# Two-layer decoder trunk: layer 0's softmax weights moved by GpSimd DMAs into fp32r transposes, layer 1's values set directly behind its scores

## The chip, the cores and the metric

The kernel runs on one core of a Trainium2 chip. The core has a matrix engine (PE), a vector engine (DVE), a scalar engine (ACT), GpSimd (POOL) and a queue that issues most DMAs (SP). The metric is the device time of one execution in microseconds.

## The reference, cut to what matters

The input is one sequence of 256 positions by 1024 features in fp32. There are two layers, each an attention and a gated feed-forward network (up-projection to 2 x 2816 columns, a causal convolution of width 3, SiLU of the gate times the value, down-projection), with RMS norms before each and residual sums behind.

Layer 0's attention is dilated: for each of 16 heads of 64 dimensions there are three groups (window, dilation) = (128, 1), (512, 4), (2048, 16), each with its own q, k and v. The three are merged by their softmax denominators, which makes one softmax over the keys of all three. Layer 1's attention is causal over one block of 256 keys. In both, q and k are normalised and partly rotated before the scores:

```python
scores = einsum('rnqhd,rnkhd->rnhqk', q, k) * HEAD_DIM ** -0.5   # masked
p = exp(scores - m);  o = (p @ v) / p.sum(-1)                     # then the heads times w_o
```

## The kernel before, in words

Every large product is made in three fp32r matmuls: a weight tile `raw` is split by ACT into a rounded part `whi` (L109) and by DVE into the rest `wlo` (L117); the activations stand as such a pair in `xT`. `mm3` (L456 to L458) adds hi x hi, lo x hi and hi x lo in PSUM. These are the product matmuls, 512 columns each.

Attention runs over four sections of four heads. A section's product is a list of pieces; each piece is one **turn**, 12 product matmuls on PE (6 in the output product). `turn()` (L218 on) fixes the program's order: around each piece it runs what tables `first`, `pre`, `mid` and `post` hold for that turn, and `at(table, dt, f)` enters a step `dt` turns from now. Inside a turn the order is: the weight splits, `first`, one split by DVE, `pre`, the piece itself, `post`. In the first 80 turns `post` is sorted by `PART`. There is no scheduler behind it: every engine works strictly in the order in which the steps were recorded.

The softmax of four heads, for each half c of the positions, goes through these steps:

- **A** (`step_A`): PE makes the scores into banks named S. There are four such banks, handed out in turn. In layer 0 one A takes all four (one per head), in layer 1 two.
- **E** (`step_E`): DVE adds the mask and takes the maximum (L716, one call and one read of `mx` per head, which is what frees the bank), ACT takes exponentials (L725) into tiles `sm`.
- **R** (`step_R`): DVE scales by the reciprocal of the sum (L733).
- **T** (`step_T`): PE transposes the weights in blocks of 128 x 128 against `ident` into S banks (L741): 12 blocks and three banks in layer 0; in layer 1 four blocks and one bank for c = 0, two times four for c = 1.
- **V** (`step_V`): ACT copies them to tiles `pT` (L748).
- **C** (`step_C`): PE multiplies with the values (L773). It uses plain fp32, in which one matmul leaves two records in the profile. For sections 0 to 2 both halves c make one group, in the last section each half its own.
- `split_T` (L433) turns C's result into the hi and lo parts of `aT` (L444 on ACT, L445 on DVE), which the output product reads.

Where these steps stand is set by numbers: `PLANS` and `C_TURN` in layer 0, and `plan`, `odd`, `last` in layer 1 (c = 0 at turn 6, 5 or 7 of the section, c = 1 two turns later). T comes four turns behind A in layer 0 (two in the last section). `OUT_ORDER` orders the pieces of the output product. q and k of a section are transposed by L580 and copied by L610 (ACT) with low parts by L616 and L618 (DVE); POOL takes the powers for the norms (L318).

Of the kernel before, what the change touches and what calls it, by code (L numbers as in the profile page):

```python
# [40 lines left out]
PART_TURNS = 80  # L41
PART = {"step_C": 0, "step_A": 1, "step_T": 2, "transpose": 3}

# [13 lines left out]


def r32(ap):
    return ap.bitcast(F32)  # L60
# [81 lines left out]
def trunk_kernel(ctx, tc, x, a_w_qkv, a_w_o, b_w_qkv, b_w_o, ffn_norm, ffn_w_up, ffn_w_down, pack, mask_a, mask_b,  # L142
# [75 lines left out]
    def turn(fn, pump=2, crowded=False):  # L218

        t = now[0]  # L220
        end = len(ws.parts) if t >= LATE else None
        n = min(pump, 1 if len(ws.parts) - ws.taken >= AHEAD else 2)
        if not crowded:
            ws.start(n)
        for f, a in first.pop(t, ()):
            f(*a)
        ws.finish(1, end)
        for f, a in pre.pop(t, ()):
            f(*a)
        if crowded:  # L230
            ws.start(n)
        ws.finish(end=end)
        if fn is not None:
            fn()

        late = post.pop(t, [])
        if t < PART_TURNS:
            late.sort(key=lambda fa: PART.get(fa[0].__name__, len(PART)))
        for f, a in late:
            f(*a)  # L240
        now[0] += 1
# [12 lines left out]
    def gain_row(l):  # L254
        g = cp.tile([P, D], F32, name="gain", bufs=1)
        nc.gpsimd.dma_start(g, ffn_norm[l:l + 1, :].to_broadcast([P, D]))
        return g
# [10 lines left out]
    for i in range(WARM):  # L268
        nc.tensor.matmul(warm[:, 0:P], plain[:, 0:P], plain[:, 0:P], start=True, stop=True)
    ident = cp.tile([P, P], F32, name="ident")  # L270
    make_identity(nc, ident)
    ones = cp.tile([P, 1], F32, name="ones")
# [8 lines left out]

    pk = cp.tile([P, PK], F32, name="pk")
    nc.sync.dma_start(pk[:, 0:264], pack[:, 0:264])
    mA = cp.tile([P, 768], F32, name="mA")
    mB = cp.tile([P, 384], F32, name="mB")
# [3 lines left out]
    cwT = [pk[:, 264 + l * 176:440 + l * 176] for l in range(2)]  # L289
    CG = cp.tile([P, 2, 4, 2, 16], F32, name="CG")  # L290
# [142 lines left out]

    def split_T(dst, k0, nk, c, src_ps, spread=False):
# [9 lines left out]
        nc.scalar.activation(hi, s, AF.Copy)  # L444
        nc.vector.tensor_sub(lo, s, r32(hi))  # L445

# [14 lines left out]
    def attention(xT, norms, ng, g0, mask):  # L461
# [198 lines left out]

        O, weights, starts = {}, {}, []

        def step_A(sec, c, heads, qkT, v, rq):
# [41 lines left out]

        def step_E(c, heads, rq, place, n, part, sm, st):
# [5 lines left out]
            these = range(len(heads))[part]  # L712
            sm.extend(t[:, i * n:(i + 1) * n] for i in range(len(these)))
            for i in these:
                s2, o = place[i]
# [11 lines left out]

        def step_R(heads, sm, st, n):
            den = st[0]
            rd = sp.tile([P, 4], F32, name="rd", bufs=2)  # L730
            nc.vector.reciprocal(rd[:, 0:len(heads)], den[:, 0:len(heads)])
            for i in range(len(heads)):
                nc.vector.tensor_scalar(sm[i], sm[i], rd[:, i:i + 1], None, op0=ALU.mult)  # L733

        def step_T(sec, c, heads, v, sm, n):
            tot = n * len(heads)
            Tp = [ps.tile([P, 512], F32, name="S", bufs=4) for _ in range((tot + 511) // 512)]
            for b in range(tot // P):
                o = b % 4 * P
                i = b * P % n  # L740
                nc.tensor.transpose(Tp[b // 4][:, o:o + P], sm[b * P // n][:, i:i + P], ident)  # L741
            at(pre, 1, step_V, sec, c, heads, v, Tp, tot)

        def step_V(sec, c, heads, v, Tp, tot):
            pT = [bp.tile([P, 768], F32, name="pT", bufs=4) for _ in range((tot + 767) // 768)]
# [7 lines left out]
            if heads[-1] < HS - 1 and (whole or not dil) or whole and c == 0:  # L753
                weights[key] = held
            else:
                at(post, starts[sec] + C_TURN[sec] - now[0] if whole and dil else 1, step_C, sec, held)

        def step_C(sec, held):

            for c, heads, pT, v in held:  # L760
# [21 lines left out]
        else:  # L782
            plan, odd, last = ([(s, 0, (0, 1, 2, 3)), (s + 2, 1, (0, 1, 2, 3))] for s in (6, 5, 7))
        pumps = PUMPS if dil else (2, 0, 0, 2, 1, 2)
        vs = [[None, None] for _ in range(NSEC)]
        for sec in range(NSEC):
            qk, v, rq = [], vs[sec], {}
            starts.append(now[0])
            for s, c, heads in last if sec == NSEC - 1 else begin if dil and sec == 0 else odd if sec % 2 else plan:
                at(post, s, step_A, sec, c, heads, qk, v, rq)  # L790
# [240 lines left out]
    at(post, 12, nc.sync.dma_start, pk[:, 264:PK], pack[:, 264:PK])  # L1031
    at(post, 20, nc.sync.dma_start, mB, mask_b)
    aT = attention(xT, norms, NG, 0, mA)
    for c in range(2):
        nc.gpsimd.dma_start(xr[:, c, :], x[0, c * P:(c + 1) * P, :])
# [109 lines left out]
```

## Time and profile before

| what | value |
|---|---|
| runs | 761.17 us median of 3 (760.97 to 761.58) |
| profiled execution | 761.35 us |
| its span, first to last instruction | 759.6 us |
| PE busy | 754.9 us, 99% |
| DVE busy | 582.4 us, 77% |
| ACT busy | 506.3 us, 67% |
| POOL busy | 68.7 us, 9% |
| DMA traffic | 133.83 MB |

A row of instruction groups reads: line of the kernel, engine, operation, output<-inputs, shape, count; in the timeline, its start and length in microseconds stand in front, and in brackets behind the idle time of the engine before it and who ended that. PEld is the loading of PE's stationary operand, which overlaps matmuls. Matmuls are pipelined: the durations of neighbours overlap, so the pace is read from start to start.

### The profile page before, as it was taken

The numbers are of one execution on the slowest core, as the hardware profiler recorded it, in microseconds if no ns is written. First come the engines' busy times: TensorE is split into PE (matmuls) and PEld (weight loads), VectorE is DVE, ScalarE is ACT, GpSimd is POOL, SyncE is SP. The second block draws the span as 40 slices with busy tenths as digits, with TensorE's granted clock in tenths as the row PEclk, the third lists the DMA queues.
The fourth block names the chain that finished last, engine by engine and source line by source line (L and its number), as shares of the span: only waits on it lengthen the run. The fifth ranks groups of instructions, "written<-read, shape, count | busy, mean of one in ns | idle before, by whom it ended". The sixth has DMA issues, their size and how long they took to land.

```text
span 759.6 us, 12047 instructions
## 1 busy us (share of the span) xinstructions
PE 754.9 (99%) x4394; PEld 634.9 (84%) x4394; DVE 582.4 (77%) x1123; ACT 506.3 (67%) x887; POOL 68.7 (9%) x77
## 2 busy tenths in 40 slices
PE   9999999999999999999999999999999999999998
PEld 7888888888888888888888888888788888888886
DVE  7887875975786566997787786979866798877874
ACT  7788666757786457676656656878765677666660
POOL 0330120320121000000000001112000000000000
PEclk9999999999999999999999999999999999999999
DMA  9947452562746436487666553743646368666621
GB/s 295 332 145 248 132 183 82 180 219 61 231 164 217 132 90 200 141 247 223 192 188 178 195 189 115 245 139 112 191 115 191 113 200 240 196 179 198 193 97 56
DMA packets 149452, 133.83 MB, mean 176 GB/s; under 512 B 5904, under 2 KB 134544, under 8 KB 149392
## 3 DMA queue, kind: packets, MB, share of 16 engines
q1 hardware_dynamic: 148816, 130.96, 56.2%
q0 software_dynamic: 576, 2.10, 0.7%
q8 instruction: 34, 0.56, 0.3%
q14 instruction: 26, 0.21, 0.1%
HBM read 131.99 MB, written 1.05 MB: 175 GB/s over the span
## 4 chain that ended last, share of the span: by engine, by line
PE 98%; DMA 1%; SPq 0%; ACT 0%; DVE 0%; issue 0%
PE acc L896 14%; PE acc L456 13%; PE acc L458 13%; PE acc L457 13%; PE acc L899 8%; PE S L949 5%; PE S L950 5%; PE S L951 5%; PE O L896 5%; PE O L899 3%; PE O L773 2%; PE S L741 2%; PE acc L513 2%; PE acc L580 2%; PE S L682 1%; PE S L458 1%
## 5 line engine op out<-in xcount | busy, mean ns | idle before, releaser
L117 DVE TENSOR_TENSOR wlo<-raw,whi 128x1024 fp32r<-128x1024 f32 x236 | 283.8, 1218 | 6.9 <-ACT whi L109 6.6
L109 ACT ACTIVATE whi<-raw 128x1024 fp32r<-128x1024 f32 x236 | 244.3, 1054 | 5.9 <-DMA raw<-in_a_w_qkv_dram 2.3
L456 PE MATMUL acc<-whi,xT 128*128 128x512 f32 x424 | 171.7, 405 | 0.0
L458 PE MATMUL acc<-wlo,xT 128*128 128x512 f32 x424 | 165.9, 391 | 0.0
L457 PE MATMUL acc<-whi,xT 128*128 128x512 f32 x424 | 165.4, 390 | 0.0
L896 PE MATMUL acc<-xT,whi 128*128 128x512 f32 x480 | 119.3, 390 | 0.0
L896 PEld LDWEIGHTS acc<-xT,whi 128*128 128x128 f32 x480 | 88.3, 188 | 17.2
L458 PEld LDWEIGHTS acc<-wlo,xT 128*128 128x128 f32 x424 | 79.6, 188 | 17.5
L456 PEld LDWEIGHTS acc<-whi,xT 128*128 128x128 f32 x424 | 79.7, 188 | 16.7 <-issue 1.2
L457 PEld LDWEIGHTS acc<-whi,xT 128*128 128x128 f32 x424 | 79.8, 188 | 14.8
L318 POOL TENSOR_TENSOR rs_y<-rs_v,mhalf 128x8 f32<-128x8 f32 x32 | 52.7, 1646 | 210.9 <-DVE rs_v L316 208.0
L899 PEld LDWEIGHTS acc<-xT,wlo 128*128 128x128 f32 x480 | 65.5, 190 | 4.7
L949 PE MATMUL S<-whi,kT 128*128 128x512 f32 x174 | 68.2, 392 | 0.0
L950 PE MATMUL S<-whi,kT 128*128 128x512 f32 x174 | 68.1, 391 | 0.0
L951 PE MATMUL S<-wlo,kT 128*128 128x512 f32 x174 | 67.7, 389 | 0.0
L920 DVE SCALAR_TENSOR_TENSOR qk<-sm,pk,qk 128x255 f32<-128x255 f32 (+1 forms) x160 | 66.7, 479 | 0.4 <-ACT qk L917 0.3
L899 PE MATMUL acc<-xT,wlo 128*128 128x256 f32 x480 | 66.9, 282 | 0.0
L909 DVE TENSOR_TENSOR sm<-acc,pT 128x256 f32<-128x256 f32 x60 | 25.4, 424 | 46.9 <-ACT pT L908 46.9
L917 ACT ACTIVATE qk<-sm,pk 128x256 f32<-128x256 f32 x80 | 47.8, 598 | 4.0 <-DVE sm L909 3.7
L933 ACT ACTIVATE kT<-qk 128x512 fp32r<-128x512 f32 x22 | 13.9, 633 | 41.2 <-DVE qk L928 41.2
L896 PE MATMUL O<-xT,whi 128*128 128x512 f32 x160 | 40.2, 393 | 0.0
L951 PEld LDWEIGHTS S<-wlo,kT 128*128 128x128 f32 x174 | 32.7, 188 | 7.0
(167 smaller groups left out, 925.7 us busy)
## 6 DMA issues: line engine op xcount, KB each, us to landing
raw<-in_ffn_w_up_dram SPq DMA_DIRECT2D x80, 512.0 KB, 4.5
raw<-in_a_w_qkv_dram SPq DMA_DIRECT2D x144, 256.0 KB, 4.4
raw<-in_ffn_w_down_dram SPq DMA_DIRECT2D x44, 512.0 KB, 4.0
raw<-in_b_w_qkv_dram SPq DMA_DIRECT2D x48, 256.0 KB, 3.5
raw<-in_a_w_o_dram SPq DMA_DIRECT2D x8, 512.0 KB, 3.4
raw<-in_ffn_w_up_dram SPq DMA_DIRECT2D x16, 256.0 KB, 3.6
raw<-in_b_w_o_dram SPq DMA_DIRECT2D x8, 512.0 KB, 4.0
xr<-in_x_dram POOLq DMA_DIRECT2D x2, 512.0 KB, 5.8
```

What stands on the lines that cost most here:

```text
L109: self.nc.scalar.activation(hi, raw, AF.Copy)
L117: self.nc.vector.tensor_sub(lo, self.raw[self.done], r32(hi))
L318: nc.gpsimd.tensor_tensor(y, v, mhalf[:, 0:n], op=ALU.pow)
L456: nc.tensor.matmul(acc, T[:, k, 0, cs], hi, start=first, stop=False)
L457: nc.tensor.matmul(acc, T[:, k, 1, cs], hi, start=False, stop=False)
L458: nc.tensor.matmul(acc, T[:, k, 0, cs], lo, start=False, stop=last)
L896: nc.tensor.matmul(acc, hi[:, k], xT[:, k].rearrange("p j t -> p (j t)"), start=(k == 0), stop=False)
L899: nc.tensor.matmul(acc[:, S:2 * S], lo[:, k], xT[:, k, 0], start=False, stop=(k == 7))
L920: nc.vector.scalar_tensor_tensor(o[:, d:S], u[:, 0:S - d], cw[:, first_tap + b:first_tap + b + 1], o[:, d:S], op0=ALU.mult, op1=ALU.add)
L949: nc.tensor.matmul(o, acts[f][:, 0, cs], hi[:, sl], start=start, stop=False)
L950: nc.tensor.matmul(o, acts[f][:, 1, cs], hi[:, sl], start=False, stop=False)
L951: nc.tensor.matmul(o, acts[f][:, 0, cs], lo[:, sl], start=False, stop=stop)
```

## The change

Layer 0, sections 0 to 2: behind R a new step M copies the tiles `sm` by GpSimd DMAs into tiles `pL` that are declared fp32r (384 KB each, two per step, so twelve in all); the bits are copied unchanged. T then transposes `pL` with an fp32r identity. T stands later: five, seven and six turns behind A for c = 0 in sections 0, 1 and 2, and six for c = 1. The last section and layer 1 keep fp32 transposes out of `sm`.

Layer 1: both score steps of section 0 stand in one turn. Values of sections 0 and 1 are entered so that they stand directly behind the next section's scores (`early`), those of section 2 behind the last section's second scores, where a new sorting of `post` puts A ahead of C. The last section's values make one group. R is entered ahead of other steps of its turn. The lo part of `aT` is made one turn after the hi part for sections 0 to 2. Two pieces of the output product change places.

To make room, the gain row takes a buffer of `kT`, the small pack one of `pT`, the two masks share one buffer, the identity is drafted in a buffer of `qk` and copied once by DVE, and layer 1's gain tables are made at turn 12, not 40.

```diff
-PART = {"step_C": 0, "step_A": 1, "step_T": 2, "transpose": 3}
+PART = {"step_C": 0, "step_A": 1, "step_T": 2, "transpose": 3}, {"step_A": 0, "step_C": 1}
...
-        if t < PART_TURNS:
-            late.sort(key=lambda fa: PART.get(fa[0].__name__, len(PART)))
+        part = PART[t >= PART_TURNS]
+        late.sort(key=lambda fa: part.get(fa[0].__name__, len(part)))
...
-        g = cp.tile([P, D], F32, name="gain", bufs=1)
+        g = bp.tile([P, D], F32, name="kT", bufs=QB)
...
-    ident = cp.tile([P, P], F32, name="ident")
-    make_identity(nc, ident)
+    draft = bp.tile([P, 512], F32, name="qk", bufs=5)[:, 0:P]
+    make_identity(nc, draft)
+    ident_r = cp.tile([P, P], F32R, name="ident")
+    nc.vector.tensor_copy(ident_r, draft)
+    ident = r32(ident_r)
...
-                at(first, 2, step_R, heads, sm, st, n)
-                at(post, 2 if sec == NSEC - 1 else 4, step_T, sec, c, heads, v, sm, n)
+                moved = [] if sec < NSEC - 1 else None
+                at(first, 2, step_R, heads, sm, st, n, moved)
+                at(post, 2 if sec == NSEC - 1 else 6 if c else (5, 7, 6)[sec], step_T, sec, c, heads, v, sm, n, moved)
                 return
-            for d, i, k in ((0, 0, 2), (2, 2, 2)) if c else ((0, 0, 4),):
-                sm, st = [], []
-                at(first, d + 1, step_E, c, heads[i:i + k], rq, place[i:i + k], n, slice(0, k), sm, st)
-                at(first, d + 2, step_R, heads[i:i + k], sm, st, n)
-                at(post, d + (3 if sec == NSEC - 1 else 2), step_T, sec, c, heads[i:i + k], v, sm, n)
+            end = sec == NSEC - 1
+            d0, d1 = (0, 1) if end else (0, 2) if sec else (1, 2)
+            steps = [(d, slice(i, i + k), [], []) for d, i, k in (((d0, 0, 2), (d1, 2, 2)) if c else ((0, 0, 4),))]
+            for d, hs, sm, st in steps:
+                at(first, d + 1, step_E, c, heads[hs], rq, place[hs], n, slice(0, len(heads[hs])), sm, st)
+                at(post, d + (3 if end else 2), step_T, sec, c, heads[hs], v, sm, n, None)
+            for d, hs, sm, st in steps:
+                mine = first.setdefault(now[0] + d + 2, [])
+                mine.insert(len(mine) if end else 0, (step_R, (heads[hs], sm, st, n, None)))
...
+            if moved is not None:
+                at(post, 0, step_M, sm, n, moved)
+
+        def step_M(sm, n, moved):
+            for i in range(0, len(sm), 2):
+                t = bp.tile([P, 768], F32R, name="pL", bufs=2)
+                moved.extend(t[:, j * n:(j + 1) * n] for j in range(2))
+                nc.gpsimd.dma_start(r32(t), box_of[id(sm[i + 1])])
...
+            src, one = (sm, ident) if moved is None else (moved, ident_r)
...
-                nc.tensor.transpose(Tp[b // 4][:, o:o + P], sm[b * P // n][:, i:i + P], ident)
-            at(pre, 1, step_V, sec, c, heads, v, Tp, tot)
+                to = Tp[b // 4][:, o:o + P]
+                nc.tensor.transpose(to if moved is None else to.bitcast(F32R), src[b * P // n][:, i:i + P], one)
+            early = not dil and sec != 2 and c and heads[-1] == HS - 1
+            at(first if early else pre, 1, step_V, sec, c, heads, v, Tp, tot, early)
...
-            whole = sec < NSEC - 1
+            whole = sec < NSEC - 1 or not dil
...
-                at(post, starts[sec] + C_TURN[sec] - now[0] if whole and dil else 1, step_C, sec, held)
+                at(post, starts[sec] + C_TURN[sec] - now[0] if whole and dil else 0 if early else 1, step_C, sec, held)
...
-                    at(first, 1, split_T, aT, sec * 2, 2, c, O[sec, c][:, c], dil)
+                    if dil:
+                        at(first, 1, split_T, aT, sec * 2, 2, c, O[sec, c][:, c], True)
+                    else:
+                        args = aT, sec * 2, 2, c, O[sec, c][:, c], False
+                        at(first, 1, split_T, *args, "h")
+                        at(first, 1 if sec == NSEC - 1 else 2, split_T, *args, "l")
...
-            plan, odd, last = ([(s, 0, (0, 1, 2, 3)), (s + 2, 1, (0, 1, 2, 3))] for s in (6, 5, 7))
+            begin, odd, plan, last = ([(s, 0, (0, 1, 2, 3)), (s + d, 1, (0, 1, 2, 3))] for s, d in ((8, 0), (5, 2), (6, 2), (7, 3)))
...
-    at(post, 40, gain_tables, 1, nc.gpsimd)
+    at(post, 12, gain_tables, 1, nc.gpsimd)
```

How it moves instructions, at three places. First, PE at the T of layer 0's section 1, first half. `S_` and a number is one use of an S bank, and in brackets stand the engines and DMA queues whose semaphores the instruction waits for. Before:

```order
L741 MATMUL S_1586<-ident_85,sm_1476 128x128 [waits DVE_49]
L741 MATMUL S_1586<-ident_85,sm_1476 128x128 x2
L741 MATMUL S_1586<-ident_85,sm_1476 128x128 [waits DVE_49]
L741 MATMUL S_1587<-ident_85,sm_1476 128x128 x2
L741 MATMUL S_1587<-ident_85,sm_1482 128x128 [waits DVE_49]
L741 MATMUL S_1587<-ident_85,sm_1482 128x128
L741 MATMUL S_1588<-ident_85,sm_1482 128x128
L741 MATMUL S_1588<-ident_85,sm_1482 128x128 [waits DVE_49]
```

After the change:

```order
L463 MATMUL acc_1651<-wlo_1554,xT_128 128x512
L762 MATMUL S_1746<-ident_90,pL_1549 128x128 [waits DMASW4_49,DVE_49]
L762 MATMUL S_1746<-ident_90,pL_1549 128x128 x3
L762 MATMUL S_1747<-ident_90,pL_1549 128x128 [waits DVE_49]
L762 MATMUL S_1747<-ident_90,pL_1549 128x128
L762 MATMUL S_1747<-ident_90,pL_1551 128x128 [waits DMASW5_49]
L762 MATMUL S_1747<-ident_90,pL_1551 128x128
L762 MATMUL S_1748<-ident_90,pL_1551 128x128 [waits DVE_49,PE_49]
L762 MATMUL S_1748<-ident_90,pL_1551 128x128 x3
```

T has moved from 24 product matmuls ahead of the scores of the second half to 12 product matmuls behind them. Before, the waits on DVE were for R, head by head; now each new bank waits for DVE, and the data for two DMAs.

Second, DVE in layer 1's section 1, between R of the first scores and the low parts of q and k (`kT`, `t_...`) that the second scores read. Before:

```order
L731 RECIPROCAL rd<-den 128x4
L733 TENSOR_SCALAR sm<-sm,rd 128x128 x4
L565 TENSOR_TENSOR qk<-qk,rs_y 128x256
L618 SCALAR_TENSOR_TENSOR kT<-acc,gqk,kT 128x2x128
L616 TENSOR_TENSOR t_5538<-acc,t_5538 128x256
L445 TENSOR_TENSOR xT<-O,xT 128x2x128 x2
L544 TENSOR_REDUCE qssq<-sq 128x8
```

After:

```order
L742 RECIPROCAL rd<-den 128x4
L744 TENSOR_SCALAR sm<-sm,rd 128x128 x4
L450 TENSOR_TENSOR xT<-O,xT 128x2x128 x2
L570 TENSOR_TENSOR qk<-qk,rs_y 128x256
L623 SCALAR_TENSOR_TENSOR kT<-acc,gqk,kT 128x2x128
L621 TENSOR_TENSOR t_5565<-acc,t_5565 128x256
L549 TENSOR_REDUCE qssq<-sq 128x8
```

The lo parts of section 0's values have moved ahead of the low parts of q and k.

Third, DVE at the start of layer 1's output product, ahead of the lo parts of section 2's values (`xT<-O,xT`). Before:

```order
L117 TENSOR_TENSOR wlo<-raw,whi 128x1024
L716 ISA sm,mx<-S,mB 128x256
L716 ISA mx 128x1
L716 ISA sm,mx<-S,mB 128x256
L716 ISA mx 128x1
L723 SCALAR_TENSOR_TENSOR nbias<-mx,rs_y 128x2
L117 TENSOR_TENSOR wlo<-raw,whi 128x1024
L731 RECIPROCAL rd<-den 128x2
L733 TENSOR_SCALAR sm<-sm,rd 128x256 x2
L445 TENSOR_TENSOR xT<-O,xT 128x2x128 x2
```

After:

```order
L727 ISA sm,mx<-S,mask 128x256
L727 ISA mx 128x1
L734 SCALAR_TENSOR_TENSOR nbias<-mx,rs_y 128x2
L727 ISA sm,mx<-S,mask 128x256
L727 ISA mx 128x1
L727 ISA sm,mx<-S,mask 128x256
L727 ISA mx 128x1
L734 SCALAR_TENSOR_TENSOR nbias<-mx,rs_y 128x2
L742 RECIPROCAL rd<-den 128x2
L744 TENSOR_SCALAR sm<-sm,rd 128x256 x2
L450 TENSOR_TENSOR xT<-O,xT 128x2x128 x2
```

The second pair of maxima has moved ahead of the lo parts, and the weight split that stood between now stands ahead of the first pair.

More of the change, by code (lines that the diff above doesn't have):

```diff
@@ L279, in trunk_kernel @@
     load_T(RAW + 1, 1)
-    pk = cp.tile([P, PK], F32, name="pk")
+    pk = bp.tile([P, 768], F32, name="pT", bufs=4)
     nc.sync.dma_start(pk[:, 0:264], pack[:, 0:264])
-    mA = cp.tile([P, 768], F32, name="mA")
-    mB = cp.tile([P, 384], F32, name="mB")
+    taps = cp.tile([P, PK - 264], F32, name="taps")
+    mA = bp.tile([P, 768], F32, name="mask", bufs=1)
     gcol = pk[:, 0:8].rearrange("p (j g) -> p j g", j=2)
@@ L288, in trunk_kernel @@
     gbf = pk[:, 136:264].rearrange("p (m d) -> p m d", d=16)
-    cwT = [pk[:, 264 + l * 176:440 + l * 176] for l in range(2)]
+    cwT = [taps[:, l * 176:176 + l * 176] for l in range(2)]
     CG = cp.tile([P, 2, 4, 2, 16], F32, name="CG")
@@ L432, in r, with split_T @@
             return self.both.rt[:, self.c:self.c + 1]
-    def split_T(dst, k0, nk, c, src_ps, spread=False):
+    def split_T(dst, k0, nk, c, src_ps, spread=False, parts="hl"):
         if spread:
@@ L443, in split_T @@
             s = src_ps[:, 0:nk * P].rearrange("p (k t) -> p k t", t=P)
-        nc.scalar.activation(hi, s, AF.Copy)
-        nc.vector.tensor_sub(lo, s, r32(hi))
+        if "h" in parts:
+            nc.scalar.activation(hi, s, AF.Copy)
+        if "l" in parts:
+            nc.vector.tensor_sub(lo, s, r32(hi))
     def new_T():
@@ L659, in v_last @@
             yield from product(done)
-        O, weights, starts = {}, {}, []
+        O, weights, starts, box_of = {}, {}, [], {}
         def step_A(sec, c, heads, qkT, v, rq):
@@ L713, in step_E @@
             sm.extend(t[:, i * n:(i + 1) * n] for i in range(len(these)))
+            box_of[id(sm[-1])] = t
             for i in these:
@@ L726, in step_E, with step_R @@
                                      scale=1.0 if dil else rq[c][:, heads[i]:heads[i] + 1], accum_out=den[:, i:i + 1])
-        def step_R(heads, sm, st, n):
+        def step_R(heads, sm, st, n, moved):
             den = st[0]
@@ L733, in step_R, with step_T @@
                 nc.vector.tensor_scalar(sm[i], sm[i], rd[:, i:i + 1], None, op0=ALU.mult)
-        def step_T(sec, c, heads, v, sm, n):
+            if moved is not None:
[5 more added lines that the diff above has]
+                nc.gpsimd.dma_start(r32(t), box_of[id(sm[i + 1])])
+        def step_T(sec, c, heads, v, sm, n, moved):
+            src, one = (sm, ident) if moved is None else (moved, ident_r)
             tot = n * len(heads)
@@ L740, in step_T, with step_V @@
                 i = b * P % n
-                nc.tensor.transpose(Tp[b // 4][:, o:o + P], sm[b * P // n][:, i:i + P], ident)
-            at(pre, 1, step_V, sec, c, heads, v, Tp, tot)
-        def step_V(sec, c, heads, v, Tp, tot):
+                to = Tp[b // 4][:, o:o + P]
+                nc.tensor.transpose(to if moved is None else to.bitcast(F32R), src[b * P // n][:, i:i + P], one)
+            early = not dil and sec != 2 and c and heads[-1] == HS - 1
+            at(first if early else pre, 1, step_V, sec, c, heads, v, Tp, tot, early)
+        def step_V(sec, c, heads, v, Tp, tot, early):
             pT = [bp.tile([P, 768], F32, name="pT", bufs=4) for _ in range((tot + 767) // 768)]
@@ L748, in step_V @@
                 nc.scalar.activation(pT[o // 768][:, o % 768:o % 768 + e - o], Tp[o // 512][:, o % 512:o % 512 + e - o], AF.Copy)
-            whole = sec < NSEC - 1
+            whole = sec < NSEC - 1 or not dil
             key = sec if whole else (sec, c)
             held = weights.pop(key, []) + [(c, heads, pT, v)]
-            if heads[-1] < HS - 1 and (whole or not dil) or whole and c == 0:
+            if heads[-1] < HS - 1 and whole or whole and c == 0:
                 weights[key] = held
             else:
-                at(post, starts[sec] + C_TURN[sec] - now[0] if whole and dil else 1, step_C, sec, held)
+                at(post, starts[sec] + C_TURN[sec] - now[0] if whole and dil else 0 if early else 1, step_C, sec, held)
         def step_C(sec, held):
@@ L788, in attention @@
             starts.append(now[0])
-            for s, c, heads in last if sec == NSEC - 1 else begin if dil and sec == 0 else odd if sec % 2 else plan:
+            for s, c, heads in last if sec == NSEC - 1 else begin if sec == 0 else odd if sec % 2 else plan:
                 at(post, s, step_A, sec, c, heads, qk, v, rq)
@@ L1027, in trunk_kernel @@
     at(post, 6, norm.sums)
-    at(post, 40, gain_tables, 1, nc.gpsimd)
+    at(post, 12, gain_tables, 1, nc.gpsimd)
     at(post, 7, norm.factors)
     at(post, 8, nc.sync.dma_start, mA, mask_a)
-    at(post, 12, nc.sync.dma_start, pk[:, 264:PK], pack[:, 264:PK])
-    at(post, 20, nc.sync.dma_start, mB, mask_b)
+    at(post, 12, nc.sync.dma_start, taps, pack[:, 264:PK])
     aT = attention(xT, norms, NG, 0, mA)
+    mB = bp.tile([P, 768], F32, name="mask", bufs=1)
+    at(post, 20, nc.sync.dma_start, mB[:, 0:384], mask_b)
     for c in range(2):
```

4 rows, old and new, of the table OUT_ORDER are left out of this document.

## The prediction

> **What bounds the kernel now.** I read the page's first parts, then the waits by engine, then the PE rows in order of time.
>
> ```profile
> span 759.6 us, 12047 instructions
> PE 754.9 (99%) x4394; PEld 634.9 (84%) x4394; DVE 582.4 (77%) x1123; ACT 506.3 (67%) x887; POOL 68.7 (9%) x77
> PEclk9999999999999999999999999999999999999999
> PE 98%; DMA 1%; SPq 0%; ACT 0%; DVE 0%; issue 0%
> ```
>
> PE is busy 99% of the span at the full granted clock, and the chain that ended last is 98% PE. So a gain must be PE time taken away, and any wait that PE does not have today is a loss of its full length. PE waits for nobody, yet the engines that feed it can be close behind; that is where a new wait would come from. Between 100 and 150 us (layer 0's attention) the waits of ACT and DVE read:
>
> ```profile
> ACT t L610 <- PE acc L580: 9.2, 3, 6.4
> DVE xT L445 <- ACT xT L444: 10.3, 2, 9.6
> ```
>
> At each section's start ACT stands at the head of its queue for up to 6.4 us until PE has transposed q and k, DVE waits behind ACT for 9.6 us, and both then work off a backlog while PE runs on.
>
> **The transposes.** The sum is made against the profiled execution, 761.35 us (span 759.6); the median of the runs, 761.17, is 0.18 lower.
>
> ```profile
> 128.26 0.39 PE L458 MATMUL acc<-wlo,xT 128*128 128x512 f32 x1
> 128.50 1.47 PE L741 MATMUL S<-ident,sm 128*128 128x128 f32 x12
> 130.04 0.40 PE L457 MATMUL acc<-whi,xT 128*128 128x512 f32 x1
> 601.01 2.00 PE L896 MATMUL acc<-xT,whi 128*128 128x512 f32 x8
> 602.86 1.12 PE L899 MATMUL acc<-xT,wlo 128*128 128x256 f32 x8
> ```
>
> From the start of the product matmul ahead of T to that of the second one behind it are 1.78 us; two product matmuls at 0.227 leave 1.33 for the twelve fp32 transposes, 0.11 each. No fp32r matmul of 128 columns is in the trace. By the last two rows, less one duration (0.390, 0.282) and over 7 steps, fp32r goes at 0.230 for 512 columns and 0.120 for 256, a straight line that gives 0.065 at 128. Half of the 256-column pace, 0.060, is the lower end; 0.109 (no gain, if the weight load sets the pace) the upper. I take 0.066: 72 transposes x 0.043 = **-3.1 us** (0 to -3.5). Section 3's 24 and layer 1's 48 transposes stay fp32.
>
> **The groups in layer 1.** What it costs to leave the product and return is read in layer 0, where values and scores stand once together and once apart:
>
> ```profile
> 231.43 0.39 PE L458 MATMUL acc<-wlo,xT 128*128 128x512 f32 x1
> 231.75 2.90 PE L773 MATMUL O<-pT,v 128*64 128x128 f32 x64
> 236.49 0.39 PE L457 MATMUL acc<-whi,xT 128*128 128x512 f32 x1
> 246.06 0.39 PE L458 MATMUL acc<-wlo,xT 128*128 128x512 f32 x1
> 248.30 0.40 PE L457 MATMUL acc<-whi,xT 128*128 128x512 f32 x1
> 251.98 0.39 PE L458 MATMUL acc<-wlo,xT 128*128 128x512 f32 x1
> 254.13 0.40 PE L457 MATMUL acc<-whi,xT 128*128 128x512 f32 x1
> ```
>
> Together (231.43 to 236.49, less 0.45): 4.61. Apart: scores 1.79 (246.06 to 248.30), half the values 1.70 (251.98 to 254.13), twice. 1.79 + 3.40 - 4.61 = 0.58 for two junctions, 0.29 each. Layer 1 gets four more junctions: scores of both halves of section 0 together, and values behind scores three times, -1.15. The last section's values, split into 8 and 16 records, become one group of 24:
>
> ```profile
> 532.86 0.39 PE L458 MATMUL acc<-wlo,xT 128*128 128x512 f32 x1
> 533.18 1.53 PE L773 MATMUL O<-pT,v 128*64 128x128 f32 x24
> 534.98 0.40 PE L457 MATMUL acc<-whi,xT 128*128 128x512 f32 x1
> 559.62 0.39 PE L458 MATMUL acc<-wlo,xT 128*128 128x512 f32 x1
> 559.94 1.09 PE L773 MATMUL O<-pT,v 128*64 128x128 f32 x16
> 561.30 0.40 PE L457 MATMUL acc<-whi,xT 128*128 128x512 f32 x1
> ```
>
> 24 records cost 2.12 - 0.45 = 1.67 and 16 cost 1.23, so 8 are 0.44 and a group's fixed part is 0.35, which goes once. Together **-1.5 us** (-0.4 if junctions inside layer 1 give nothing, to -1.8).
>
> **What T waits for in section 1.** The moved T of the first half stands one turn behind the scores of the second half, which fill all four banks "S"; T needs three of them, in the order in which step E frees them. E's order on DVE is unchanged, so its times of today count:
>
> ```profile
> 117.76 0.38 ACT L610 ACTIVATE t<-acc 128x256 f32<-128x256 f32 x1 [6.40 <-PE acc L580]
> 135.39 0.97 PE L682 MATMUL S<-kT 64*128 64x256 f32 x12
> 140.03 0.08 DVE L716 DVE_READ_ACCUMULATOR2_ANT mx<- 128x1 f32 x1
> 143.04 0.08 DVE L716 DVE_READ_ACCUMULATOR2_ANT mx<- 128x1 f32 x1
> 140.20 0.39 PE L456 MATMUL acc<-whi,xT 128*128 128x512 f32 x1
> ```
>
> (The second row is those scores; the last is the first matmul after the turn behind them, where T will stand. Of the two reads at 140.03 and 143.04 the first frees the first bank, the second the third bank.) DVE's backlog hangs on PE only through the release at 117.76; two cheaper Ts lie before it, so it comes 1.04 earlier: banks at 139.07 and 142.08. PE is earlier by the same 1.04 and by the 1.33 of a T that it has not yet done: 140.20 - 2.37 = 137.83. Unhindered the third bank's transposes would start at 137.83 + 8 x 0.066 = 138.36, but may not before 142.08: **+3.7 us**. A wait cannot gain, so the lower end is 0; the upper is 4.8, were E no earlier than today. I take the worked value, since every link in it is a row. Sections 0 and 2 have no scores between E and T.
>
> **What DVE is late for in layer 1.** In section 1 the second scores need the low half of q:
>
> ```profile
> 509.54 0.42 DVE L616 TENSOR_TENSOR t<-acc,t 128x256 fp32r<-128x256 f32 x1
> 510.60 0.43 DVE L445 TENSOR_TENSOR xT<-O,xT 128x256 fp32r<-128x256 f32 x1 [0.64 <-ACT xT L444]
> 510.65 0.97 PE L682 MATMUL S<-kT,t 64*128 64x256 f32 x12
> ```
>
> It is done at 509.96 for PE's 510.65: 0.69 spare. The change puts two such xT subtractions (0.43 each) ahead of it and lets PE come 0.29 sooner by the junction: short by 0.4 to 0.9, say 0.6. At the output product the low half of section 2's values is the late one:
>
> ```profile
> 549.51 1.23 DVE L117 TENSOR_TENSOR wlo<-raw,whi 128x1024 fp32r<-128x1024 f32 x1
> 551.75 0.42 DVE L445 TENSOR_TENSOR xT<-O,xT 128x256 fp32r<-128x256 f32 x1
> 553.78 0.50 PE L456 MATMUL acc<-whi,xT 128*128 128x512 f32 x1
> ```
>
> PE takes it at 553.78, 1.6 after it is done. Between the scores and that use PE loses the separate 8 records and two groups' fixed parts (1.6 in all), while DVE gets the weight split of 549.51 and one more pair of maxima ahead of it, in part under ACT's exponentials: 0.9 later. Short by 0.4 to 1.2, say 0.8. Both: **+1.4 us** (0 to 2.1).
>
> **What costs nothing.** POOL issues twelve DMAs more; today's xr issue is the only one to price them by:
>
> ```profile
> 229.31 1.32 POOL L1035 DMA_DIRECT2D xr<-in_x_dram  x2
> xr<-in_x_dram POOLq DMA_DIRECT2D x2, 512.0 KB, 5.8
> ```
>
> 12 x 0.66 = 8 us on an engine that is 9% busy. Behind each pair only the next power (L318) is queued, and behind that a rescale on DVE that PE needs two turns later. The one identity copy on DVE lies before the first weights land; the gain tables only move on POOL; gain row, pack and masks in shared buffers wait for readers long done. The 384 KB copies share the DMA engines with the weights; if that cover went, it would be the DMA rival below, one microsecond of PE for each that a landing is late.
>
> **Sum.** -3.1 - 1.5 + 3.7 + 1.4 = +0.5: 761.85 for the profiled execution, **761.7** as a median.
>
> **Rivals.** *No bank wait*: E is early enough, because ACT no longer copies T's result ahead of the second exponentials. Against it: DVE is busy 15.81 us of the 16.00 between 127 and 143, so an earlier ACT moves nothing:
>
> ```profile
> 127.00:143.00 16.00, 15.81 (x33) 1.00 0.64 194
> ```
>
> (the columns: stretch, length, DVE busy, instructions, granted clock, DMA share and GB/s). Without the wait it would be 761.7 - 3.7 = 758.0, faster.
>
> *The weight load sets the transposes' pace*: each loads 128 new columns for a 128-column pass. For it: nowhere does PE load fp32r weights more often than every 0.120 us. Against it: the 16 records of 559.94 go at (1.09 - 0.28)/15 = 0.054, each with 64 columns of weights; in the 64 records of 231.75 half are such, 1.73, and the rest take 2.90 - 0.22 - 1.73 = 0.95, or 0.030 per 64 columns loaded, 0.06 per 128. It decides from 0.066 up; halfway to 0.109 the gain falls by 72 x 0.022 = 1.6: 763.3, slower. [...]
>
> *The DMA lands late*: section 2's first T moves by 24 product matmuls.
>
> ```profile
> 182.51 1.41 DVE L733 TENSOR_SCALAR sm<-sm,rd 128x384 f32<-128x384 f32 x4
> 184.10 1.47 PE L741 MATMUL S<-ident,sm 128*128 128x128 f32 x12
> ```
>
> The weights are ready at 183.92 and T comes at 184.10 + 24 x 0.227 = 189.6; the second DMA, issued 0.66 later and needed 0.4 later, has 5.4 us. The xr pair took 5.8 in the median for 512 KB from HBM. Beyond 5.4 each microsecond is one of PE's; at 6.8, +1.4: 763.1, slower. [...]
>
> **Chances.** The forecast 0.50, own range 760.3 to 763.2; no bank wait 0.15; weight load 0.15; late DMA 0.15; anything else 0.05. A measurement of this kernel tells 0.2% (1.5 us) from no change, so same is 759.65 to 762.7. Faster: 0.13 from the first rival, 0.05 from the forecast's lower edge and the rest, 0.18. Slower: 0.08 of the forecast, 0.11 of each of the last two, 0.02 of the rest, 0.32. Same 0.50. The range 758.6 to 764.0 leaves out about a tenth on each side: half of the first rival's lower part below, the harder half of a slow pace or a late landing above.
>
> **What would show it.** Right: transposes from pL at about 0.066 each, in groups of twelve of some 0.8 us; PE with its first wait since the start, 3 to 4 us, at the T behind section 1's second scores, ended by DVE's maxima (the line of step E), most of it before the ninth transpose; two waits under 1.2 us in layer 1 ended by DVE. Wrong: PE still 99% busy with no wait there (first rival), transposes at 0.09 or more (second), or PE waits ended by a DMA into pL (third).

## The result, and the profile after

The changed kernel takes 765.95 us (median of 6 runs, 765.36 to 766.79) against 761.38 us (6 runs, 760.97 to 761.58): the ratio is 1.0061, 95% interval 1.0051 to 1.0071. It is slower, by three times the 0.2% that a measurement tells, and 1.95 us above the upper end of the predicted range. The profiled executions differ by 4.42 us (765.77 and 761.35), their spans by 4.4.

The page of the changed kernel, the lines that answer to those shown of before:

```profile
span 764.0 us, 12091 instructions
PE 754.8 (99%) x4394; PEld 635.0 (83%) x4394; DVE 582.4 (76%) x1124; ACT 505.8 (66%) x887; POOL 74.2 (10%) x89
PE 88%; DVE 6%; ACT 3%; issue 2%; DMA 1%; POOL 0%; DVEq 0%; SPq 0%; ACTq 0%; POOLq 0%
pL<-sm POOLq DMA_DIRECT2D x12, 384.0 KB, 4.7
```

PE's busy time is as before to 0.1 us (shorter transposes and a stretch at half clock, both below, go into it), while the span grew by 4.4. The chain that ended last was 98% PE; now 10% of it is DVE, ACT and DMA. So PE is no longer alone on the path. Its waits:

```profile
PE S L762 <- DVE mx L727: 3.2, 2, 2.1
PE S L269 <- DVE qk L266: 1.0, 1, 1.0
PE S L687 <- DVE t L621: 0.9, 1, 0.9
PE acc L462 <- DVE xT L450: 0.4, 1, 0.4
```

The second row is the start of the program, which waits as long before the change. The other three are the waits that the prediction named, at its places and ended by its engine. None is ended by a DMA into pL.

The first of them, PE in order of time at the T of layer 0's section 1, first half:

```profile
138.16 0.39 PE L463 MATMUL acc<-wlo,xT 128*128 128x512 f32 x1
139.69 1.01 PE L762 MATMUL S<-ident,pL 128*128 128x128 f32 x8 [1.14 <-DVE mx L727]
142.79 0.59 PE L762 MATMUL S<-ident,pL 128*128 128x128 f32 x4 [2.09 <-DVE mx L727]
143.18 0.76 PE L461 MATMUL acc<-whi,xT 128*128 128x512 f32 x1
143.73 0.63 PE L462 MATMUL acc<-whi,xT 128*128 128x512 f32 x1
146.62 0.39 PE L463 MATMUL acc<-wlo,xT 128*128 128x512 f32 x1
```

1.14 us before the first transpose, 2.09 us before the ninth. Measured as the prediction measures a group (138.16 to 143.73, less 0.45) the place costs 5.12 us, of which T itself is 1.06 and 0.24 belongs to a slowed product matmul behind it: the bank wait is 3.8 us. (The idle time in the brackets is 0.6 less, 3.2: it leaves out the overlap of neighbours that PE loses at each of the two stops.) Then something new: the product matmuls behind the wait go at 0.43 us, not 0.227. From 143.18 to 146.62 are eight steps in 3.44 us; at the usual pace they take 1.90 (0.31 for the first, 0.227 for the others). That is **1.5 us** more. The clock shows why (columns: stretch, length, busy time and instructions of PE, PEld, DVE, ACT, POOL, granted clock, DMA share, GB/s):

```profile
138.00:143.00 5.00, 1.77 (x14) 1.16 (x12) 4.96 (x13) 1.31 (x4) 0.00 (x0) 1.00 0.67 211
143.00:146.40 3.40, 3.40 (x12) 2.72 (x11) 1.96 (x9) 3.04 (x9) 0.00 (x0) 0.51 0.52 158
146.40:150.00 3.60, 3.60 (x19) 3.00 (x18) 3.48 (x9) 2.58 (x6) 2.60 (x3) 0.99 0.02 5
```

PE worked 1.77 of the 5.00 us up to 143.00, and for the next 3.4 us its clock is 0.51, then 0.99. The idle pieces ahead of that were 1.14 and 2.09 us long, with 1.0 us of transposes between.

The transposes out of pL, in a group without a wait:

```profile
70.37 0.39 PE L463 MATMUL acc<-wlo,xT 128*128 128x512 f32 x1
70.60 1.14 PE L762 MATMUL S<-ident,pL 128*128 128x128 f32 x12
71.58 0.47 PE L461 MATMUL acc<-whi,xT 128*128 128x512 f32 x1
71.88 0.40 PE L462 MATMUL acc<-whi,xT 128*128 128x512 f32 x1
```

70.37 to 71.88, less 0.45: 1.06 us for twelve, 0.088 each, where fp32 took 1.33 and 0.11. Six groups bring 6 x 0.27 = 1.6 us.

Layer 1, in order: the second scores of section 1, the output product, and the norm behind it.

```profile
513.45 0.38 PE L687 MATMUL S<-kT,t 64*128 64x256 f32 x2
514.77 0.86 PE L687 MATMUL S<-kT,t 64*128 64x256 f32 x10 [0.94 <-DVE t L621]
515.56 0.66 PE L762 MATMUL S<-ident,sm 128*128 128x128 f32 x4
556.15 0.50 PE L461 MATMUL acc<-whi,xT 128*128 128x512 f32 x1
557.07 0.50 PE L462 MATMUL acc<-whi,xT 128*128 128x512 f32 x1 [0.42 <-DVE xT L450]
571.83 1.31 PE L338 MATMUL acc<-ident,qk 128*128 128x128 f32 x8
572.90 0.48 PE L461 MATMUL acc<-whi,xT 128*128 128x512 f32 x1
580.05 0.63 PE L338 MATMUL acc<-ident,qk 128*128 128x128 f32 x4
580.44 0.47 PE L461 MATMUL acc<-whi,xT 128*128 128x512 f32 x1
```

Before the change, the group behind the scores (which start at 510.65, a row of the prediction) and the norm:

```profile
511.56 0.66 PE L741 MATMUL S<-ident,sm 128*128 128x128 f32 x4
565.18 1.03 PE L335 MATMUL acc<-ident,qk 128*128 128x128 f32 x8
565.97 0.48 PE L456 MATMUL acc<-whi,xT 128*128 128x512 f32 x1
```

The twelve scores took 0.91 us from their start to the next group (510.65 to 511.56), now 2.11 (513.45 to 515.56): 1.20 us, of which 0.94 is idle time. From 556.15 to 557.07 are 0.92 us, where a step behind such a change of work takes 0.34: 0.58. And the norm's transposes: the first group took 0.79 us to the next product matmul before the change (565.18 to 565.97), now 1.07 (571.83 to 572.90). The second group stands 0.48 us behind the product matmul ahead of it (its start 579.57), not 0.23. With the first step behind it that is **0.55 us** for both, which the prediction did not have.

### The profile page after: what moved, and what is told of

The parts are those of the page before. It is cut to its first block, busy times and chain, and to the rows that moved or that the text cites. A ratio compares the mean times of both kernels' runs of the same rounds, so it can differ in the third digit from the quotient of the medians.

```text
span 764.0 us, 12091 instructions
## 1 busy us (share of the span) xinstructions
PE 754.8 (99%) x4394; PEld 635.0 (83%) x4394; DVE 582.4 (76%) x1124; ACT 505.8 (66%) x887; POOL 74.2 (10%) x89
## 4 chain that ended last, share of the span: by engine, by line
PE 88%; DVE 6%; ACT 3%; issue 2%; DMA 1%; POOL 0%; DVEq 0%; SPq 0%; ACTq 0%; POOLq 0%
PE acc L923 14%; PE acc L461 10%; PE acc L463 10%; PE acc L462 10%; PE acc L926 7%; PE S L976 5%; PE S L977 5%; PE S L978 5%; PE O L923 5%; PE O L926 2%; PE acc L518 2%; DVE wlo L117 2%; PE S L762 2%; PE O L795 2%; PE acc L585 1%
## 5 line engine op out<-in xcount | busy, mean ns | idle before, releaser
L947 DVE SCALAR_TENSOR_TENSOR qk<-sm,taps,qk 128x255 f32<-128x255 f32 (+1 forms) x160 | 66.7, 479 | 0.4 <-ACT qk L944 0.3
L944 ACT ACTIVATE qk<-sm,taps 128x256 f32<-128x256 f32 x80 | 47.8, 598 | 4.1 <-DVE sm L936 3.9
```

The costliest lines, as they stand in the source:

```text
L947: nc.vector.scalar_tensor_tensor(o[:, d:S], u[:, 0:S - d], cw[:, first_tap + b:first_tap + b + 1], o[:, d:S], op0=ALU.mult, op1=ALU.add)
```

## The experiments

**Theory.** The loss is the bank wait (3.8), a clock that is halved, to 0.51, because PE idled in it (1.5), and in layer 1 three places at which DVE is late (2.3); the gains are 1.6 for the transposes and about 1.4 for the groups. Rivals: the halved clock has another cause; PE waits in section 1 for something else than the banks; layer 1 is about even; the pace of the transposes is not set by the weight load. The first four runs share 19 runs of the kernel before (761.35 us), the next four share 27 (761.51), the last two 20 (761.41).

**T one turn later.** The first half of section 1 transposes two turns behind the second scores:

```diff
-at(post, 2 if sec == NSEC - 1 else 6 if c else (5, 7, 6)[sec], step_T, sec, c, heads, v, sm, n, moved)
+at(post, 2 if sec == NSEC - 1 else 6 if c else (5, 8, 6)[sec], step_T, sec, c, heads, v, sm, n, moved)
```

> Edit: T of layer 0's section 1, first half, two turns behind the second scores instead of one. Theory (bank wait, then a halved clock because PE idled): PE reaches T 2.7 us later, at about 141.2 us; the third bank is freed near 142.7, so the idle time falls from 3.2 us to about 0.8 and the granted clock stays at 1.00. Time 765.95 - 2.4 - 1.5 = 762.0 us. Rival A (the halved clock has nothing to do with the idle time, it comes with the new fp32r transposes or the DMAs): the clock still falls to 0.5 behind this T, 763.5 us. Rival B (T waits for the DMA or something else than the banks): no change, 765.9 us.

Measured: 762.93 us, ratio 1.002 (1.0011 to 1.0029).

```profile
PE acc L585 <- DVE kT L621: 1.4, 1, 1.4
PE S L762 <- DVE mx L727: 0.9, 1, 0.9
143.00:146.40 3.40, 3.40 (x20) 2.91 (x19) 1.96 (x9) 3.11 (x9) 0.00 (x0) 1.00 0.50 155
```

The bank wait fell from 3.2 to 0.9 us and the clock stayed at 1.00 in the same stretch: rivals A and B are out. 3.0 us came back of the 3.9 expected, because of a new wait of 1.4 us at the transposes of q and k (L585), which the next run shows more plainly.

**Section 1's first half as before.**

```diff
-moved = [] if sec < NSEC - 1 else None
+moved = [] if sec < NSEC - 1 and (sec, c) != (1, 0) else None
-at(post, 2 if sec == NSEC - 1 else 6 if c else (5, 7, 6)[sec], step_T, sec, c, heads, v, sm, n, moved)
+at(post, 2 if sec == NSEC - 1 else 6 if c else (5, 4, 6)[sec], step_T, sec, c, heads, v, sm, n, moved)
```

> Edit: only the first half of layer 0's section 1 is handled as before (fp32 transposes out of sm, four turns behind its scores, no DMA); the other five keep pL. Theory: no wait and no halved clock in layer 0, one group of twelve transposes 0.26 us dearer. Time 765.95 - 3.8 - 1.5 + 0.3 = 760.9 us. Rival (the loss in layer 0 is spread, or comes from the DMAs' traffic): 763 us or more.

Measured: 762.11 us, ratio 1.0009 (1.0000 to 1.0018). Bank wait and slow clock are gone, but 1.2 us are missing against the expectation. PE and DVE of this kernel at the transposes of q and k:

```profile
148.69 0.69 DVE L570 TENSOR_TENSOR qk<-qk,rs_y 128x512 f32<-128x512 f32 x1
149.53 0.63 PE L585 MATMUL acc<-ident,qk 128*128 128x128 f32 x4 [1.20 <-DVE qk L570]
```

The same place before the change:

```profile
149.02 1.47 PE L741 MATMUL S<-ident,sm 128*128 128x128 f32 x12
149.55 0.69 DVE L565 TENSOR_TENSOR qk<-qk,rs_y 128x512 f32<-128x512 f32 x1
150.39 0.63 PE L580 MATMUL acc<-ident,qk 128*128 128x128 f32 x4
```

Before, DVE is done with `qk` at 150.24 and PE takes it at 150.39, because the T of section 1's second half stands in front from 149.02. The change moves that T away. PE then reaches L585 1.2 us before DVE has finished; DVE works off its backlog (15.72 of the 16 us from 127 to 143) and cannot be earlier. In the changed kernel itself the wait does not show: PE comes there some 4 us later, from the bank wait and the slow clock.

**Filling the wait.** 24 matmuls of the same block, whose results are overwritten, ahead of the fifth transpose, in the time in which PE idled; once as transposes, once as plain fp32r matmuls:

```diff
+if moved is not None and (sec, c, b) == (1, 0, 4):
+    for _ in range(24):
+        nc.tensor.transpose(to.bitcast(F32R), src[b * P // n][:, i:i + P], one)
+        # or: nc.tensor.matmul(to, src[b * P // n][:, i:i + P], one, start=True, stop=True)
```

> Edit: the wait stays, but PE is given 24 more transposes of the same pL block (2.1 us at 0.088 each) between the eighth and the ninth transpose of that T, where it idled 2.09 us; they are overwritten. Theory (the clock is halved because PE idled): banks come free at the same times, the granted clock stays 1.00 behind it, time 765.95 - 1.5 = 764.4 us. Rival A (clock halved by something else): still 0.5 for 3.4 us, 765.9 us. Rival B (transposes do not count as activity): also 765.9 us, but then the same filling with plain matmuls cures it.

> Edit: as the filling with 24 transposes, but with 24 plain fp32r matmuls of the same block against the identity. Theory (the clock is halved because PE idled): granted clock 1.00 behind the wait, 764.4 us. Rival A (clock halved by something else): 765.9 us. If the filling with transposes leaves the clock halved and this one does not, transposes do not count as activity.

With transposes 764.77 us (764.03 to 765.6, ratio 1.0046, 1.0029 to 1.0063), a span of 762.6 against 764.0. PE of this kernel:

```profile
139.83 0.54 PE L765 MATMUL S<-ident,pL 128*128 128x128 f32 x4 [1.13 <-DVE mx L727]
140.31 2.23 PE L764 MATMUL S<-ident,pL 128*128 128x128 f32 x24
142.37 1.06 PE L765 MATMUL S<-ident,pL 128*128 128x128 f32 x8
143.27 0.46 PE L461 MATMUL acc<-whi,xT 128*128 128x512 f32 x1
143.57 0.39 PE L462 MATMUL acc<-whi,xT 128*128 128x512 f32 x1
143.80 0.40 PE L463 MATMUL acc<-wlo,xT 128*128 128x512 f32 x1
```

The next product matmul starts at 143.27, 143.18 without the filling, and DVE's read for the third bank ends at 142.79, 142.64 without it, so the banks came free at nearly the same times. But the pace behind is 0.23, the granted clock 1.00 throughout, and the span is 1.4 us shorter. So it was the idleness that halved the clock (0.51 without the filling), not the fp32r transposes or the DMAs, and in this execution 24 transposes in 2.06 us of it (140.31 to 142.37) kept the clock at 1.00. With plain matmuls the clock of the profiled execution also stayed at 1.00, with a span of 763.0.

The filling did not keep the clock in every execution. The mean granted clock of the four timed runs is 0.999, 1.0, 0.997 and 1.0 with transposes, and 1.0, 0.995, 0.996 and 1.0 with plain matmuls; it is 0.996 or 0.998 in all six of the changed kernel and 0.999 or 1.0 in all ten of the run with T one turn later. The runs with 0.995 and 0.996 took 768.31 and 767.44 us, the other two with plain matmuls 764.79 and 765.71, so their median of 766.58 shows no saving. Only the profiled executions left a trace; where the others lost the clock is not known.

**What sets the transposes' pace.** In the changed kernel, three other ways to transpose a block (its one run of 770.47 us does more work, and its time is not compared):

```diff
+# section 0: two plain matmuls of 64 identity columns, all 128 columns of weights each
+nc.tensor.matmul(to[:, r * 64:r * 64 + 64], blk, one[:, r * 64:r * 64 + 64], start=True, stop=True)
+# section 1, second half: one plain matmul, and two more with 64 columns of weights
+nc.tensor.matmul(to, blk, one, start=True, stop=True)
+nc.tensor.matmul(to[0:64], blk[:, 0:64], one, start=True, stop=True)
+# section 2: one plain matmul
+nc.tensor.matmul(to, blk, one, start=True, stop=True)
```

> Edit on the changed kernel, three kinds of transposition by matmul, all into the same banks: in section 0 each block of pL as two plain matmuls of 64 identity columns (24 per group, full weights each); in section 1's second half one plain matmul per block and two more with only 64 columns of weights that write the lower half again; in section 2 one plain matmul in place of the transpose. Theory W (the loading of 128 columns of weights sets 0.088 us): 24 x 0.088 = 2.1 us for section 0's groups, 12 x 0.088 + 24 x 0.044 = 2.1 for section 1's. Theory M (the 128 columns that pass set it): 24 x 0.044 to 0.05 = 1.1 to 1.2 us and 36 x 0.088 = 3.2 us. Section 2: 1.06 us if it is not the transposing mode, about 0.8 (12 x 0.066, the forecast's pace) if it is.

```profile
69.92 2.76 PE L765 MATMUL S<-ident,pL 128*128 128x64 f32 x24
72.51 0.49 PE L461 MATMUL acc<-whi,xT 128*128 128x512 f32 x1
161.84 0.28 PE L770 MATMUL S<-ident,pL 128*64 128x128 f32 x2
161.96 0.28 PE L768 MATMUL S<-ident,pL 128*128 128x128 f32 x1
197.71 1.45 PE L773 MATMUL S<-ident,pL 128*128 128x128 f32 x12
199.00 0.45 PE L461 MATMUL acc<-whi,xT 128*128 128x512 f32 x1
```

With all 128 columns of weights, a pass of only 64 columns goes at 2.59 / 24 = 0.108 us, one of 128 columns at 1.29 / 12 = 0.107: halving what passes saves nothing. With 64 columns of weights two passes of 128 take 0.12, 0.06 each. So the weight load sets the pace of the plain matmul, about 0.11 us for 128 columns, and theory M is out. Theory W had the size wrong: the price that it took, 0.088, belongs to the transpose alone. A transpose is cheaper than the plain matmul that does the same, 0.082 by this measure (70.60 to 71.58) against 0.107. That the weight load also sets the pace of the transposing form, at a faster rate, is the author's nearest reading; it was not measured with fewer columns, and why it would load faster is open. The run also repeats the two bank waits (1.12 and 2.09 us of idle time), and behind them the product matmuls go at 0.43 us again, from 146.49 to 148.19.

**Section 1 as before, whole.** This is the base of all later runs; it has neither bank wait nor slow clock.

```diff
-moved = [] if sec < NSEC - 1 else None
+moved = [] if sec in (0, 2) else None
-at(post, 2 if sec == NSEC - 1 else 6 if c else (5, 7, 6)[sec], step_T, sec, c, heads, v, sm, n, moved)
+at(post, 2 if sec == NSEC - 1 else 4 if sec == 1 else 6 if c else 5 + sec // 2, step_T, sec, c, heads, v, sm, n, moved)
```

> Edit: both halves of layer 0's section 1 as before (fp32 transposes out of sm, four turns behind their scores, no DMA); sections 0 and 2 keep pL. Theory (with only the first half put back, PE waited 1.2 us for DVE's scaling of qk, because the second half's T no longer stood ahead of that wait as cover): that wait goes, T costs 0.3 more, 762.11 - 1.2 + 0.3 = 761.2 us. Rival (DVE is late there whatever PE does ahead of it): the wait stays, 762.4 us.

Measured: 761.21 us, ratio 0.9997 (0.9988 to 1.0006). The wait at L585 is gone, as the theory has it. Putting section 1 back recovers 4.7 us: the 3.8 and 1.5, less the 0.5 that its two groups had gained.

**The same without layer 1's part.** Score order, grouping, R, low parts and output pieces of layer 1 as before (its core):

```diff
-begin, odd, plan, last = ([(s, 0, (0, 1, 2, 3)), (s + d, 1, (0, 1, 2, 3))] for s, d in ((8, 0), (5, 2), (6, 2), (7, 3)))
+plan, odd, last = ([(s, 0, (0, 1, 2, 3)), (s + 2, 1, (0, 1, 2, 3))] for s in (6, 5, 7))
...
-early = not dil and sec != 2 and c and heads[-1] == HS - 1
+early = False
...
-whole = sec < NSEC - 1 or not dil
+whole = sec < NSEC - 1
...
-at(first, 1, split_T, *args, "h")
-at(first, 1 if sec == NSEC - 1 else 2, split_T, *args, "l")
+at(first, 1, split_T, *args)
```

> Edit: section 1 as before, and all of layer 1 as before too (orders, groups, low parts, output pieces); left are pL and fp32r transposes in sections 0 and 2. Theory (layer 1's part costs more than it brings: junctions -1.1, waits on DVE +0.9 and +0.6, the norm behind the output product +0.5, together +0.9): 761.2 - 0.9 = 760.3 us. The forecast's reading (layer 1's part about even, -0.1): 761.3 us.

Measured: 760.24 us, ratio 0.9984 (0.9975 to 0.9993). So layer 0's part in sections 0 and 2 is a gain of 1.3 us (four groups at 0.27 make 1.1), and layer 1's part loses 0.97 us. With its three late places at 1.20 + 0.58 + 0.55 = 2.33, its groups bring 2.33 - 0.97 = 1.4. (The expectation took the idle time, 0.9, for the first place and so had 1.1.) This is a remainder; no run measures the groups alone.

**DVE's order in layer 1.** First attempt:

```diff
-at(first, 1, split_T, *args, "h")
-at(first, 1 if sec == NSEC - 1 else 2, split_T, *args, "l")
+if sec == 2:
+    split_T(*args, "h")
+    mine = first.setdefault(now[0] + 2, [])
+    i = next((i for i, (f, a) in enumerate(mine) if f is step_R), len(mine))
+    mine.insert(i, (split_T, (*args, "l")))
+else:
+    at(first, 1, split_T, *args, "h")
+    at(post if sec < 2 else first, 2 if sec < 2 else 1, split_T, *args, "l")
...
-at(post, 3, norms[c].transpose, 0)
-at(post, 3, norms[c].transpose, 1)
+at(post, 3 + l, norms[c].transpose, 0)
+at(post, 3 + l, norms[c].transpose, 1)
```

> Edit: section 1 as before; layer 1 keeps its new groups, but the low parts of sections 0's and 1's values are made behind the low parts of q and k, the high part of section 2's values directly behind C on ACT and its low part ahead of R, and the norm's transposes of the first half one turn later. Theory (the three waits come from the order on DVE alone): the waits of 0.9 and 0.4 us go, and the first late norm transposes, 761.2 - 1.6 = 759.6 us. Rival (DVE is short of time there, and its next step is late instead, as in layer 0): 760.7 us or more.

Measured: 761.76 us, ratio 1.0004 (0.9995 to 1.0013): no gain, by its number the rival's. But the waits say otherwise. Those on DVE fell to 0.3 (t, L621) and 0.2 (xT, L450), and two new ones are ended by ACT's copies L448: 0.5 us inside C, whose second half waited for the copy of the first, and 1.0 us at the start of the feed-forward network, which needs the norm's first half right behind, so that its transposes cannot come a turn later. Both were made by the edit. Second attempt, the same steps behind the whole of step C, and the norm's transposes left where they were:

```diff
-                if heads[-1] == HS - 1:
...
+            for c in () if dil else sorted({h[0] for h in held}):
+                args = aT, sec * 2, 2, c, O[sec, c][:, c], False
+                if sec == 2:
+                    split_T(*args, "h")
...
```

> Edit: as the run with section 1 as before, and in layer 1 the low parts of sections 0's and 1's values behind the low parts of q and k, the high parts of section 2's values on ACT directly behind the whole of C (not between its halves, where C's second half waited 0.5 us for it), their low parts ahead of R; the norm's transposes stay where the change has them (one turn later PE waited 1.0 us for their copies). Theory (the two waits on DVE in layer 1 come from the order alone): 761.21 - 0.7 - 0.7 = 759.8 us, with the late norm transposes (0.5) still in it. Rival (DVE is short of time there): no gain, 761 us or more.

Measured: 759.5 us (759.29 to 759.97), ratio 0.9976 (0.9967 to 0.9985). The waits that are left, the first two at the start of the program:

```profile
PE S L269 <- DVE qk L266: 1.0, 1, 1.0
PE acc L518 <- ACT whi L96: 0.5, 1, 0.5
PE S L687 <- DVE t L621: 0.3, 1, 0.3
```

The order was the cause, though 0.3 us of idle time is left at the scores. This kernel beats both: 0.24% faster than before the change.

**The last section's values in two groups again,** with the old order of the output product's pieces:

```diff
-(1, (0, 5)), (1, (1, 1)), (1, (1, 2)), (1, (0, 6)), (1, (0, 7)), ...
+(1, (0, 5)), (1, (0, 6)), (1, (0, 7)), (1, (1, 1)), (1, (1, 2)), ...
-whole = sec < NSEC - 1 or not dil
+whole = sec < NSEC - 1
```

> Edit: the former, and the last section's values in two groups with the old order of the output product's pieces. Theory (the norm behind the output product is late because two pieces were exchanged): its two groups of transposes cost 0.88 and 0.45 us again instead of 1.16 and 0.7, the extra group costs 0.3 to 0.6; 759.8 - 0.5 + 0.5 = 759.8 us. Rival (the norm is late for another reason, the waits on PE ahead of it or DVE's splits): the norm's groups stay dear and the time is 760.3 us.

Measured: 759.72 us, ratio 0.9979 (0.9970 to 0.9988). The norm's groups cost 0.88 and 0.45 us again, against 1.16 and 0.71 in the run above. The edit puts pieces and groups back together, so it does not tell which of the two made the norm late, but the traces show the step. DVE, at the sum for piece (0, 7), which ends the first half's residual sum; the run above, then this one:

```profile
560.74 1.22 DVE L117 TENSOR_TENSOR wlo<-raw,whi 128x1024 fp32r<-128x1024 f32 x1
561.87 0.69 DVE L858 TENSOR_TENSOR xr<-acc,xr 128x512 f32<-128x512 f32 x1
559.48 0.69 DVE L858 TENSOR_TENSOR xr<-acc,xr 128x512 f32<-128x512 f32 x1 [0.45 <-PE acc L463]
```

The transposes stand three pieces behind (0, 7) in both orders, and from the start of the sum to the last scaled `qk` the chain takes 4.1 us in both. But in the exchanged order a weight split stands ahead of the sum, and DVE takes it up 0.42 us after PE has finished (0, 7) at 561.45; here it waits for PE and takes it up at once. In the changed kernel it is 0.42 too (567.91 to 568.33), and 0.53 at the second half's last sum. Before the change PE also had a group of values, 16 records, between (0, 7) and the transposes as cover. One group for the last section saves about as much as the late norm costs; the two kernels' times do not differ.

## Why the prediction was wrong

The forecast was +0.5 us, measured are +4.42 on the same kind of execution. Term by term:

| term | forecast | measured or worked out |
|---|---|---|
| 72 transposes in fp32r | -3.1 | -1.6 |
| bank wait in section 1 | +3.7 | +3.8 |
| slow clock behind it | not there | +1.5 |
| groups of layer 1 | -1.5 | -1.4 (a remainder) |
| DVE late in layer 1 | +1.4 | +1.8 (1.20 and 0.58) |
| norm behind the output product | not there | +0.55 |
| DMAs on POOL | 0 | 0 (no wait of PE ends with one) |
| sum | +0.5 | +4.65 |

(0.2 us between this sum and 4.42 are not assigned.)

**The mechanism of the forecast's largest loss was right,** and so was its size: T waits in section 1 for banks that E frees, in two pieces, the larger one before the ninth transpose. (The first and the ninth transpose started 0.6 to 0.7 us behind the bank times worked out, and PE came 0.55 later than worked out, since the transposes ahead had gained less; the difference stayed.) The first rival, no wait there, is refuted by the row of 3.2 us, the third, a late DMA, by its absence: the copies landed after 4.7 us in the median, and no wait of PE ends with one. The two waits in layer 1 were where the prediction put them; 1.20 lies above its "0.4 to 0.9", 0.58 in the lower part of its "0.4 to 1.2", and both together, 1.8, inside its "0 to 2.1".

**The first step that failed is the price of a wait.** "any wait that PE does not have today is a loss of its full length" is how the prediction priced every wait: at its own length. Here a PE that idled 3.2 us within 5 paid a second time, 1.5 us, through its clock, which fell to 0.51; the sum had no term for that and no rival named it. The runs show it from both sides: filled idle time (1.00 in the profiled execution, same banks), and a shorter wait (0.9 us, 1.00).

**The second is "I take 0.066".** The straight line from 512 and 256 columns to 128 takes the pass as the only cost; a plain matmul of 128 columns took 0.107 us and one of 64 no less, so there the weight load is longer than the pass, and for the transposes this is the author's nearest reading. That was the second rival, at 0.15, and in size it came true to its halfway mark: 0.088. The trace of before spoke against it only by fp32 rows with 64 columns of weights, from which 0.06 us per 128 was worked out; the plain fp32r matmuls of the pace run took 0.107 with 128. This is worth 1.5 us.

**The third is a change that was not priced.** "Two pieces of the output product change places" stood in the description of the change and in no term. The late norm cost 0.55 us. The question to ask is the one asked for T: who is late next? The norm's chain starts at the last of the moved pieces, and DVE came to its sum 0.42 us late, with a weight split ahead of it.

**A cover was taken away unseen.** The T of section 1's second half hid DVE's lateness at the transposes of q and k, with 0.15 us to spare. The prediction looked at where T went, not at what stood behind its old place. It cost nothing in the changed kernel, since PE was already late, but it is why removing the bank wait alone brings 762.11 and not 760.9.

Added up: the forecast with the second rival's 1.6 is 763.3, inside the range; with the clock it is 764.8, outside, and with the norm 765.4.

## What to carry to other kernels

When a moved step gets a wait on an engine that was never idle, price the wait, then ask how much idle time falls together: here 3.2 us within 5 cost 1.5 us more through the matrix engine's clock (0.51 for 3.4 us), and single waits of 0.9 to 1.4 us did not (a mean clock of 1.0 in the profiled executions). When a step is moved, check both places: what it waits for at the new one, and what it hid at the old one. Here plain matmuls with 128 columns of weights took no less time when half as many columns passed (0.108 us with 64, 0.107 with 128), and the transposes 0.088 where the pass alone was taken for 0.066, so the faster type was worth half of what its passes said.

## What the runs showed of the hardware

- Transposes by matmul, 24 of them as filler in a wait of 2.1 us, kept the granted clock at 1.00 in that stretch of the profiled execution (mean 0.999); the mean was 1.0 in two of the other three and 0.997 in the last.
- Behind 3.2 us of PE idle in two pieces (1.14 and 2.09, 1.0 us of transposes between) the clock was 0.51 for 3.4 us, and in the pace run, behind 1.12 and 2.09, the product matmuls again went at 0.43 us, not 0.227; with single waits of 0.9, 1.2 and 1.4 us the profiled executions show a mean clock of 1.0. Where the limit lies between was not measured.
- fp32r with 128 columns of weights: 0.107 to 0.108 us per plain matmul, whether 64 or 128 columns pass; 0.06 with 64 columns of weights and 128 that pass; 0.082 to 0.088 as a transpose.
- Copies of 384 KB from SBUF to SBUF issued by GpSimd landed after 4.7 us in the median beside the weights' traffic, and delayed nothing that a run shows.
